# The second part of an output projection in two passes of 256 columns, with the column sums and the first FFN pair built group by group

## The chip, the cores and the metric

The kernel runs on one core of one Trainium2 chip. The metric is the device time of one execution in microseconds (us). The kernel before has a median of 2437.38 us in three runs (2435.72 to 2438.55).

The engines are called by short names: PE multiplies matrices, DVE, ACT and POOL work on tiles by element, and SP issues nearly all transfers, one after the other, in the order of the program.

## The reference, cut to what matters

One layer of a hybrid decoder, for 2048 prompt tokens and 8 decode tokens, in fp32, with a model width of 1024 and an FFN width of 2816:

```python
z = rms_norm(x, norm_mix_g) @ w_in                      # attention and convolution branches from z
...
h = x + jnp.concatenate([attn_o, conv_o], axis=-1) @ w_out
fg, fu = jnp.split(rms_norm(h, norm_ffn_g) @ w_ffn_in, 2, axis=-1)
ffn_ext = jnp.concatenate([ffn_hist.astype(fg.dtype), fg], axis=1)
fc = causal_dwconv(ffn_ext, ffn_conv_w, ffn_conv_b)
h = h + (jax.nn.gelu(fc, approximate=False) * fu) @ w_ffn_out
gate = jax.nn.sigmoid(rms_norm(h, norm_ple_g) @ w_ple_gate)
h = h + (p @ w_ple_proj) * gate
```

The change lies between `h = x + ... @ w_out` and `... @ w_ffn_in`. The norm in between needs, for each token, the sum of the squares of all 1024 entries of h: a sum over all eight blocks of 128 rows of h, which is held transposed (channels on partitions, tokens in columns).

## The kernel before, in words

**Products.** Every fp32 operand is split into a high and a low part (`hilo`, L212 to L213: ACT casts the high part, DVE subtracts it), and each product is three matmuls (L195 to L197). A weight arrives as a raw tile of 128x1024 (512 KB, L106), is split into a `whl` tile, and is used from there.

**The stream of weights.** Class `W` holds the whole sequence of weights in the order of their use. `W.topup` splits up to three weights ahead (three `whl` buffers) and loads two further ahead (two `raw` buffers). Its loads stand on SP's queue between all other loads and stores.

**Halves and columns.** The tokens are worked in two halves of 1024 columns (half 1 has 8 decode columns more). For each half, the output projection runs over columns 0 to 511 first (called the first part here, operand `mixA` or `mixB`), then over the rest, the second part. Half 0's second part is one piece of 512 columns, half 1's has pieces of 256 and 264 (`C1`).

**One unit of the second part** (`w_out_unit`, m = 0 to 7, one weight each): load the residual x (`xr`), eight times three matmuls per piece into `wo`, transpose x on PE into `xres`, copy it into `hst` (ACT), add the product (DVE, L798), store `hst` to `h` in DRAM (L806), and add its squares to the column sums `acc` (ACT squares into `sqh`, DVE adds, L816). In the last unit the squares stay apart (`tail`) and the sums take them in directly. Beside the units, `w_out_second` makes the sums of the first part: `stats` (L747 to L754: matmuls with ones, a copy, and POOL's power) at m = 0, `bcast` of the inverse root into `rb` at m = 1, and then `hn_k` for each block k: load h's columns 0 to 511 back, multiply by gain and `rb` (L773), and split into `Rb` (names `bA`, `bB`), which hold the normalised first 512 columns; `b11` keeps four of them unsplit. In half 0 the decode attention (`dec_step`) runs beside these units.

**The first part of the FFN.** The operand is taken as 2x2 blocks (rows 0 to 511 and 512 to 1023 of the normalised h; columns 0 to 511 and the rest), and the weights likewise; seven block products replace eight. Of a unit (`ffn_in`, two weights of 512 KB), `first` makes two products, X and Y, that need only `Rb`; `second` makes five, with the operands T1, T2, T3, B22 and T4, which are sums of blocks. Three of the weights are sums too, made by DVE in `topup` (L138 to L141).

`build_T` makes the five operands, once per half, for all 512 (half 1: 520) columns: loads of h into `tB` (L1120, L1122), for each k a scaling (L1134, L1138), a difference (L1135, L1139, L1143, L1150 and L1151) and a split (L1130 on ACT, L1131 on DVE): 48 DVE instructions and 20 ACT copies in all. Then come the `second` products of units 0 and 1, and units 2 to 21.

`ffn_in_all` sets the order after the last unit: `stats` and `bcast` of the last columns, `first` of units 0 and 1, `build_T`, `second` of units 0 and 1, then the units from 2 on. In half 0 a convolution (L411, DVE) fills gaps from there on (`start_conv`).

## Time and profile before

| what | us |
|---|---|
| median of three runs | 2437.38 |
| the profiled execution | 2442.29 |
| its span | 2440.5 |
| second part of the output projection, half 0 | 579.4 to 634.5 |
| first two FFN units, half 0 | 634.5 to 694.2 |
| later 20 units, half 0 | 694.2 to 1094.4 |
| second part of the output projection, half 1 | 1402.0 to 1457.0 |
| first two FFN units, half 1 | 1457.0 to 1518.7 |
| later 20 units, half 1 | 1518.7 to 1927.6 |

PE is busy for 2349.3 us of the span (96%), DVE for 1734.4 (71%), ACT for 1188.4 (49%) and POOL for 290.1 (12%). A busy time counts an instruction from its start to its end; instructions follow one another in a pipeline, so the distance from one start to the next, not the length of one, tells what one more of them costs. In a row of the timeline, the first number is the start, the second the duration, and what stands in brackets is how long the engine stood idle before and what released it. Times in the rest of the document are those of the span's clock.

### The profile page before, as it was taken

To read this page: it belongs to the slowest core of one execution; us is meant where nothing else is said; L and a number is where in the kernel's file an instruction comes from. 1 tells how busy PE (TensorE), PEld (TensorE's weight loads), DVE (VectorE), ACT (ScalarE), POOL (GpSimd) and SP (SyncE) were. 2 spreads that over 40 slices of the span, in tenths; PEclk is the share of its full clock that TensorE was granted. 3 is DMA by queue.
4 is the path that set the end of the run, shared out by engine and by line. 5 is a ranking of instruction groups with operands and counts; after the bars stand their busy time and mean duration, and the time that the engine had idled before them with its cause. 6 is when DMAs were issued, how large, how long until landed. Compare 5 with 4: busy or idle time off the path is not lost.

```text
span 2440.5 us, 36702 instructions
## 1 busy us (share of the span) xinstructions
PE 2349.3 (96%) x13709; PEld 2035.6 (83%) x13709; DVE 1734.4 (71%) x2932; ACT 1188.4 (49%) x2186; POOL 290.1 (12%) x358
## 2 busy tenths in 40 slices
PE   7899999999899999999999998999999999999999
PEld 6777778877677777778778797999999999988889
DVE  4889879856799999779944469666666654465553
ACT  4566666665444444464333345444444543344443
POOL 3312232200011121110001002111111000000000
PEclk9999999999899999999999999999999999999999
DMA  8434332267322222355556661222222665666663
GB/s 293 168 113 138 136 96 73 81 213 228 113 87 83 83 86 84 91 168 189 191 166 190 201 187 57 79 78 78 77 82 79 207 213 180 200 215 201 201 188 114
DMA packets 357076, 348.19 MB, mean 143 GB/s; under 512 B 24414, under 2 KB 277784, under 8 KB 352770
## 3 DMA queue, kind: packets, MB, share of 16 engines
q1 hardware_dynamic: 336610, 333.25, 43.4%
q10 hardware_dynamic: 20288, 12.60, 1.8%
q8 instruction: 107, 1.75, 0.3%
q14 instruction: 71, 0.58, 0.1%
HBM read 271.61 MB, written 75.78 MB: 142 GB/s over the span
## 4 chain that ended last, share of the span: by engine, by line
PE 66%; DVE 17%; DMA 8%; ACT 4%; issue 3%; POOL 2%; SPq 0%; ACTq 0%; DVEq 0%
DVE co L411 5%; PE X L195 5%; PE X L196 5%; PE X L197 5%; PE fo L197 5%; PE fo L196 5%; PE fo L195 5%; DVE whl L213 3%; PE Z L195 2%; PE Z L196 2%; PE Z L197 2%; PE pg L195 2%; PE pg L196 2%; PE pg L197 2%; PE wo L195 2%
## 5 line engine op out<-in xcount | busy, mean ns | idle before, releaser
L213 DVE TENSOR_TENSOR whl<-raw,whl 128x1024 fp32r<-128x1024 f32 (+1 forms) x314 | 361.3, 1151 | 240.7 <-ACT whl L212 240.1
L212 ACT CAST whl<-raw 128x1024 fp32r<-128x1024 f32 (+1 forms) x314 | 310.0, 987 | 257.7 <-PE fo L197 135.8
L411 DVE SCALAR_TENSOR_TENSOR co<-gi,cvec,co 128x512 f32<-128x512 f32 x480 | 367.0, 788 | 2.9
L197 PE MATMUL fo<-act,whl 128*128 128x512 f32 (+2 forms) x880 | 308.5, 351 | 2.2 <-DVE whl L213 2.1
L195 PE MATMUL fo<-act,whl 128*128 128x512 f32 (+2 forms) x880 | 308.2, 350 | 1.9 <-DVE hs L1305 1.9
L196 PE MATMUL fo<-act,whl 128*128 128x512 f32 (+2 forms) x880 | 309.0, 351 | 0.0
L197 PEld LDWEIGHTS fo<-act,whl 128*128 128x128 f32 x880 | 165.4, 188 | 19.5 <-DVE whl L213 3.3
L195 PE MATMUL X<-T,whl 128*128 128x512 f32 (+2 forms) x528 | 173.3, 330 | 8.2 <-ACT whl L212 2.5
L195 PEld LDWEIGHTS fo<-act,whl 128*128 128x128 f32 x880 | 165.4, 188 | 17.6 <-DVE hs L1305 2.3
L196 PEld LDWEIGHTS fo<-act,whl 128*128 128x128 f32 x880 | 165.6, 188 | 15.9 <-issue 0.5
L196 PE MATMUL X<-T,whl 128*128 128x512 f32 (+2 forms) x528 | 172.3, 327 | 2.6 <-DVE T L1131 2.6
L197 PE MATMUL X<-T,whl 128*128 128x512 f32 (+2 forms) x528 | 170.8, 324 | 0.6 <-DVE whl L213 0.6
L1228 POOL TENSOR_TENSOR snB<-snB 128x256 f32<-128x256 f32 (+1 forms) x66 | 87.1, 1320 | 549.4 <-ACT snB L1219 549.4
L1181 ACT ACTIVATE ft<-ft 128x512 f32<-128x512 f32 (+2 forms) x110 | 60.2, 548 | 170.3 <-DVE ft L1176 129.8
L195 PEld LDWEIGHTS X<-T,whl 128*128 128x128 f32 x528 | 100.8, 192 | 24.5 <-ACT snA L1192 6.7
L195 PE MATMUL ag<-r,whl 128*128 128x512 f32 (+2 forms) x320 | 116.5, 366 | 0.0
L196 PE MATMUL ag<-r,whl 128*128 128x512 f32 (+2 forms) x320 | 115.0, 360 | 0.0
L197 PE MATMUL ag<-r,whl 128*128 128x512 f32 (+2 forms) x320 | 113.6, 355 | 0.0
L1173 ACT ACTIVATE ft<-ext,fvec 128x512 f32<-128x512 f32 (+2 forms) x110 | 80.0, 728 | 64.6 <-DVE ext L1195 32.7
L196 PEld LDWEIGHTS X<-T,whl 128*128 128x128 f32 x528 | 101.2, 192 | 11.2 <-DVE T L1131 4.0
L197 PEld LDWEIGHTS X<-T,whl 128*128 128x128 f32 x528 | 101.2, 192 | 9.1 <-DVE whl L213 1.1
L212 ACT CAST act<-act 128x512 fp32r<-128x512 f32 (+2 forms) x110 | 56.4, 535 | 73.9 <-DMA act<-actd 72.9
(382 smaller groups left out, 6400.8 us busy)
## 6 DMA issues: line engine op xcount, KB each, us to landing
raw<-in_w_ffn_out SPq DMA_DIRECT2D x110, 512.0 KB
raw<-in_w_ffn_in SPq DMA_DIRECT2D x88, 512.0 KB
whl<-agd SPq DMA_DIRECT2D x24, 1024.0 KB
hs<-h SPq DMA_DIRECT2D x80, 256.0 KB
raw<-in_w_out SPq DMA_DIRECT2D x32, 512.0 KB
raw<-in_w_ple_gate SPq DMA_DIRECT2D x32, 512.0 KB
actd<-ft SPq DMA_DIRECT2D x44, 256.0 KB
act<-actd SPq DMA_DIRECT2D x44, 256.0 KB
```

Of the source, the lines that this page charges most:

```text
L195: PE.matmul(ps, wh, xh, start=first, stop=False, skip_group_check=more)
L196: PE.matmul(ps, wh, xl, start=False, stop=False, skip_group_check=more)
L197: PE.matmul(ps, wl, xh, start=False, stop=last, skip_group_check=more)
L212: AC.copy(hi, src)
L213: DV.tensor_tensor(lo, src, hi.bitcast(F32), op=ALU.subtract)
L411: DV.scalar_tensor_tensor(co[c], t[:, i:i + QT], cvec[:, c, i:i + 1], co[c], op0=ALU.mult, op1=ALU.add)
L1173: AC.activation(t[:, :n], ext[:, 2 + o:2 + o + n], func=AF.Identity, scale=w2, bias=bi)
L1181: AC.activation(t[:, :n], t[:, :n], func=AF.Gelu)
L1228: GP.tensor_tensor(s3, s3, s5, op=ALU.add)
```

## The change

The second part of the projection is run as two passes over all eight weights. The first pass makes columns 512 to 767 (`ga`), the second columns 768 to 1023 (`gb`, with the 8 decode columns in half 1). The weights of `w_out` stand in the stream three times per half instead of two, which is eight more loads and splits of 512 KB per half. In the first pass the residual shares the tile `hst`. The sums of `ga` are made at m = 0 of the second pass, its `bcast` at m = 1, its loads into `tB` at m = 0, and its first eight steps of the T operands (T1 and T2) from m = 2 on. `hn_k` stays in the first pass.

`build_T` becomes a class, `BuildT`, whose `step(i, o, n)` makes step i of 20 for one column group; the same 20 steps run for each group, on half the width. After the passes: sums of `gb`, `first` of units 0 and 1 over the full width, steps 8 to 15 of `ga`, the middle part of unit 0 (four products) for `ga`, steps 0 to 15 of `gb`, unit 0's middle for `gb`, steps 16 to 19 (T4) of both, unit 0's last product for both, and unit 1's `second` at full width as before. The decode steps that ran after the units of half 0 now run between the passes.

```diff
-    for _ in range(2):
+    for _ in range(3):
         for m in range(KD):
             W.add(col(w_out, m * 128))
...
+    C2 = [[(512, 256), (768, 256)], [(512, 256), (768, 264)]]
...
-        xr = xpool() if xpool else P2["st"].tile([128, STW], F32, tag="st", name="xr")
+        ho = P2["st"].tile([128, STW], F32, tag="st", name="hst")
+        if hi - lo <= 264 and not xpool:
+            xr = ho[:, RW:]
+        else:
+            xr = xpool() if xpool else P2["st"].tile([128, STW], F32, tag="st", name="xr")
...
+        ga, gb = C2[half]
         for m in range(KD):
-            w_out_unit(half, R, m, C1[half], acc, xs, xpool, tail if m == KD - 1 else None)
+            w_out_unit(half, R, m, [ga], acc, None, None, tail if m == KD - 1 else None)
             step()
...
+        if between:
+            between()
+        bt = BuildT(half, Rb, rb, b11, *where)
+        for m in range(KD):
+            w_out_unit(half, R, m, [gb], acc, xs, lambda: s2_tile("xr"), tail if m == KD - 1 else None)
+            if m == 0:
+                stats(acc, rt, *ga, tail)
+                bt.load(*ga)
+            if m == 1:
+                bcast(rt, rb, *ga)
+            for k in spread(m, 2, 8):
+                bt.step(k, *ga)
...
+        def load(self, o, n):
+            c = slice(o - 512, o - 512 + n)
+            for a, d in ((1, 0), (0, 4)):
+                for k in range(4):
+                    SY.dma_start(self.tmp[k][:, a, c], hd[self.half][k + d][:, o:o + n])
...
+            if j < 2:
+                v = (b12, b22)[j]
+                DV.scalar_tensor_tensor(v, v, gains[:, 1, k + 4 * j:k + 4 * j + 1], self.rb[:, o:o + n],
+                                        op0=ALU.mult, op1=ALU.mult)
+            if j == 0:
+                DV.tensor_tensor(t1, b12, t1, op=ALU.subtract)
+                self.split(self.T1[k], t1, c)
+            elif j == 1:
+                DV.tensor_tensor(t2, b22, t1, op=ALU.subtract)
+                self.split(self.T2[k], t2, c)
+            elif j == 2:
+                DV.tensor_tensor(b12, b22, b12, op=ALU.subtract)
+                self.split(self.T3[k], b12, c)
+            elif j == 3:
+                self.split(self.B22[k], b22, c)
+            else:
+                DV.tensor_tensor(t2, b21[:, 0, c].bitcast(F32), t2, op=ALU.subtract)
+                DV.tensor_tensor(t2, t2, b21[:, 1, c].bitcast(F32), op=ALU.add)
+                self.split(self.T4[k], t2, c)
...
-        RT = build()
+        bt.load(*gb)
+        for i in range(8, 16):
+            bt.step(i, *ga)
+        cols = [(o - 512, n, x0[-1 if i else 0], o - 512 if len(gs) == 1 else 0) for i, (o, n) in enumerate((ga, gb))]
+        u0.mid(*cols[0], bt.T2, bt.T1, bt.T3, bt.B22, True)
+        for i in range(16):
+            bt.step(i, *gb)
+        u0.mid(*cols[1], bt.T2, bt.T1, bt.T3, bt.B22, True)
+        for g in (ga, gb):
+            for i in range(16, 20):
+                bt.step(i, *g)
+        RT = bt.done()
...
+        for i, c in enumerate(cols):
+            u0.end(*c, bt.T4, i == 1)
+        u0.finish(ns)
+        for g, X in zip(gs, x1):
+            u1.second(*g, X, RT, True)
+        u1.finish(ns)
```

A scheduler places the instructions, so the order on each engine shows what the diff alone does not. On DVE in half 0, around the last residual add (the last row with `hst`; `rt` is the copy of the token sums, `ext<-Y` belongs to unit 0's `first`, `s1f` and `raw` without `whl` are weight sums), before:

```order
L213 TENSOR_TENSOR whl<-raw,whl 128x1024
L816 TENSOR_TENSOR accA<-accA,sqh 128x512
L213 TENSOR_TENSOR whl<-s1f,whl 128x512
L213 TENSOR_TENSOR whl<-raw,whl 128x512
L798 TENSOR_TENSOR hst<-hst,wo 128x512
L754 COPY rt_5549<-st 128x4
L138 TENSOR_TENSOR s1f<-raw 128x512
L139 TENSOR_TENSOR raw<-raw 128x512
L1195 TENSOR_TENSOR ext<-Y,snA 128x512
L213 TENSOR_TENSOR whl<-raw,whl 128x1024
L1134 SCALAR_TENSOR_TENSOR tB<-tB,gains,rb 128x512
```

and now (L1161 scales, L1167 makes T2's difference, L1147 splits):

```order
L802 TENSOR_TENSOR hst<-hst,wo 128x256
L213 TENSOR_TENSOR w_6894<-raw,w_6894 128x512
L213 TENSOR_TENSOR whl<-raw,whl 128x1024
L213 TENSOR_TENSOR whl<-s1f,whl 128x512
L213 TENSOR_TENSOR whl<-raw,whl 128x512
L1161 SCALAR_TENSOR_TENSOR tB<-tB,gains,rb 128x256 x2
L1167 TENSOR_TENSOR t2f<-tB,b_6303 128x256
L1167 TENSOR_TENSOR t2f<-tB,b_6309 128x256
L755 COPY rt_5549<-st 128x2
L1222 TENSOR_TENSOR ext<-Y,snA 128x512
L1147 TENSOR_TENSOR T_6500<-t2f,T_6500 128x256
L1147 TENSOR_TENSOR T_6501<-t2f,T_6501 128x256
```

The splits of unit 0's weights and the end of T2 for the first column group now stand between the last residual add and the copy of the sums; before, the copy followed the add at once.

On DVE, half 0, at the end of the T operands (`T` is T4, `ft` is the gate of unit 0), before:

```order
L1131 TENSOR_TENSOR T_6699<-t2f,T_6699 128x512
L1151 TENSOR_TENSOR t2f<-t2f,bA 128x512
L1221 TENSOR_TENSOR ext<-Z,snA 128x512
L141 TENSOR_TENSOR raw<-raw 128x512
L1131 TENSOR_TENSOR T_6700<-t2f,T_6700 128x512
L1175 SCALAR_TENSOR_TENSOR ft<-ext,fvec,ft 128x512 x2
L213 TENSOR_TENSOR whl<-raw,whl 128x1024
```

and now:

```order
L1176 TENSOR_TENSOR t2f<-t2f,bA 128x256
L1202 SCALAR_TENSOR_TENSOR ft<-ext,fvec,ft 128x256
L138 TENSOR_TENSOR s1f<-raw 128x512
L1147 TENSOR_TENSOR T_7182<-t2f,T_7182 128x256
L1203 SCALAR_TENSOR_TENSOR ft<-ext,fvec,ft 128x256
L139 TENSOR_TENSOR raw<-raw 128x512
L1202 SCALAR_TENSOR_TENSOR ft<-ext,fvec,ft 128x256
L140 TENSOR_TENSOR raw<-s1f,raw 128x512
L1203 SCALAR_TENSOR_TENSOR ft<-ext,fvec,ft 128x256
L141 TENSOR_TENSOR raw<-raw 128x512
L1258 TENSOR_TENSOR ft<-ft,X 128x256
```

The last of unit 1's weight sums, L141, stood ahead of the last split of T4; now L139 to L141 stand behind it.

On SP, half 0, where the second pass begins (`h_7` is the last block of the first pass; `tB` are the loads of h for the first column group), now:

```order
L106 DMA raw<-in_w_out 128x8x128
L810 DMA h_7_73<-hst 128x256
L1046 DMA mixB<-dOc 64x4x8
L106 DMA raw<-in_w_out 128x8x128
L1046 DMA mixB<-dOc 64x4x8
L789 DMA xr<-in_x_prompt 128x2x128
L106 DMA raw<-in_w_out 128x8x128
L1143 DMA tB<-h_0_66 128x256
L1143 DMA tB<-h_1_67 128x256
...
L789 DMA xr<-in_x_prompt 128x2x128
L106 DMA raw<-in_w_out 128x8x128
```

Where the last store of the second part was followed by the `tB` loads of 512 columns and by FFN weights, three more loads of `w_out` stand around that store now, and the next one stands behind the first group's `tB` loads.

More of the change, by code (lines that the diff above doesn't have):

```diff
@@ L180, in hybrid_layer_kernel @@
         if half:
-            for _ in range(2):
+            for _ in range(3):
                 for m in range(KD):
@@ L1076, in hybrid_layer_kernel, with w_out_second @@
     tail = {}
-    def w_out_second(half, R, acc, rt, Rb, step, xs=None, xpool=None):
+    def w_out_second(half, R, acc, rt, Rb, step, where, xs=None, between=None):
         rb = st_tile("rb")
@@ new lines, in w_out_second, with end_decode @@
+        if between:
[10 more added lines that the diff above has]
+                bt.step(k, *ga)
+        return rb, bt
+    def end_decode():
+        for _ in range(20):
+            dec_step()
+        dec_st.close()
+        RP[2] = ctx.enter_context(tc.tile_pool(name="R2", bufs=1, side="right", reuse_waits="tile"))
@@ L1242, in ffn_in, with ffn_in_all @@
         u = FfnIn()
-        u.first, u.second, u.finish = first, second, finish
+        u.first, u.second, u.finish, u.mid, u.end = first, second, finish, mid, end
         return u
-    def ffn_in_all(half, Rb, rb, acc, rt, build, ns, start=None):
+    def ffn_in_all(half, Rb, rb, acc, rt, bt, ns, start=None):
         gs = GROUPS[half]
-        stats(acc, rt, 512, sum(c for _, c in C1[half]), tail)
-        with later(72 if half else 33):
-            for o, c in C1[half]:
-                bcast(rt, rb, o, c)
+        ga, gb = C2[half]
+        stats(acc, rt, *gb, tail)
+        with later(72 if half else 60):
+            bcast(rt, rb, *gb)
         u0 = ffn_in(half, Rb, 0)
```

118 lines of the change are left out of this document (48 added, 70 removed).

## The prediction

> **What bounds the kernel now.** I read the table of engines by stretch first, over the four stretches that the change touches and the twenty FFN-in units behind each pair. Columns: length, busy time of PE, weight load, DVE, ACT, POOL, then granted clock, DMA share, GB/s.
>
> ```profile
> 579.40:634.50 55.10, 52.25 (x267) 40.67 (x265) 37.66 (x62) 29.62 (x48) 2.14 (x3) 1.00 0.71 210
> 634.50:694.20 59.70, 51.43 (x193) 36.34 (x193) 52.77 (x82) 26.69 (x44) 6.28 (x7) 0.89 0.27 85
> 1402.00:1457.00 55.00, 55.00 (x450) 53.50 (x449) 35.03 (x61) 26.63 (x53) 2.49 (x4) 1.00 0.63 191
> 1457.00:1518.70 61.70, 50.82 (x360) 46.90 (x360) 52.93 (x93) 31.76 (x61) 15.62 (x11) 0.92 0.18 54
> 694.20:1094.40 400.20, 395.49 (x1695) 315.70 (x1694) 363.95 (x518) 187.14 (x280) 63.35 (x61) 1.00 0.31 95
> 1518.70:1927.60 408.90, 406.00 (x3362) 403.67 (x3361) 258.78 (x482) 195.65 (x388) 45.35 (x79) 1.00 0.28 86
> ```
>
> Second part of the output projection (rows 1 and 3): PE nearly full at full clock, DVE 35 to 38 of 55 us, DMA at 0.63 to 0.71. First pair (rows 2 and 4): 59.7 and 61.7 us, while a later pair takes 400.2/10 = 40.0 and 408.9/10 = 40.9. So 19.7 and 20.8 us are lost, 40.5 in all; more than that cannot be won.
>
> The timeline names what ends last there: half 0, DVE from its last residual add on (start, us, then idle before and releaser in brackets), and PE at the end.
>
> ```profile
> 634.56 0.68 DVE L798 TENSOR_TENSOR hst<-hst,wo 128x512 f32<-128x512 f32 x1
> 638.96 0.16 DVE L754 COPY rt<-st 128x4 f32<-128x4 f32 x1 [3.72 <-PE st L747]
> 640.78 0.69 DVE L138 TENSOR_TENSOR s1f<-raw 128x512 f32<-128x512 f32 x1 [1.66 <-DMA raw<-in_w_ffn_in]
> 642.83 0.69 DVE L1195 TENSOR_TENSOR ext<-Y,snA 128x512 f32<-128x512 f32 x1 [0.62 <-DMA tB<-h]
> 643.85 1.23 DVE L213 TENSOR_TENSOR whl<-raw,whl 128x1024 fp32r<-128x1024 f32 x1 [0.33 <-ACT whl L212]
> ...
> 677.70 0.68 DVE L1131 TENSOR_TENSOR T<-t2f,T 128x512 fp32r<-128x512 f32 x1
> ```
>
> ```profile
> 679.02 0.50 PE L195 MATMUL X<-T,whl 128*128 128x512 f32 x1
> 694.24 0.39 PE L195 MATMUL X<-bA,whl 128*128 128x512 f32 x1
> ```
>
> DVE idles 3.72 + 1.66 + 0.62 + 0.33 = 6.3 us, then works without a gap until the last split of T4 (677.70); behind it PE needs 16 us for what is left of the first pair, and unit 2 starts at 694.24. PE meanwhile runs thin, and its clock falls:
>
> ```profile
> 650.00:660.00 10.00, 7.05 (x19) 3.62 (x17) 9.94 (x17) 4.11 (x8) 0.00 (x0) 0.79 0.00 0
> 660.00:670.00 10.00, 8.33 (x19) 5.65 (x19) 9.88 (x18) 5.71 (x11) 0.00 (x0) 0.53 0.00 0
> ```
>
> Half 1 has the same shape:
>
> ```profile
> 1457.35 0.42 DVE L798 TENSOR_TENSOR hst<-hst,wo 128x264 f32<-128x264 f32 x1
> 1497.82 0.70 DVE L1131 TENSOR_TENSOR T<-t2f,T 128x520 fp32r<-128x520 f32 x1
> ```
>
> ```profile
> 1502.09 0.58 PE L195 MATMUL X<-T,whl 128*128 128x256 f32 x1 [2.54 <-ACT whl L212]
> 1518.73 0.28 PE L195 MATMUL X<-bB,whl 128*128 128x256 f32 x1
> ```
>
> The bound of the first pair is therefore DVE's list between the last residual add and the last T4 split. The change must shorten that list, and pays in a stage where PE is full.
>
> **The list, counted.** Prices are distances between starts of back-to-back DVE instructions:
>
> ```profile
> 666.90 2.49 DVE L1131 TENSOR_TENSOR B<-tB,B 128x512 fp32r<-128x512 f32 x4
> 669.31 0.68 DVE L1151 TENSOR_TENSOR t2f<-t2f,bA 128x512 f32<-128x512 f32 x1
> ```
>
> ```profile
> 1428.39 0.41 DVE L798 TENSOR_TENSOR hst<-hst,wo 128x256 f32<-128x256 f32 x1
> 1428.72 0.75 DVE L773 SCALAR_TENSOR_TENSOR hs<-hs,gains,rb 128x512 f32<-128x512 f32 x1
> 1429.38 0.42 DVE L816 TENSOR_TENSOR accB<-accB,sqh 128x256 f32<-128x256 f32 x1
> ```
>
> A 512-wide tensor_tensor takes 2.41/4 = 0.60 us, a 256-wide one 0.33, a 512-wide scalar_tensor_tensor 0.66 (256 wide: 0.33 + 0.06 = 0.39, an estimate); a 1024-wide split 1.23 (row 643.85). In the order of instructions, before, half 0, 47 + 8 instructions of 512 and one of 1024 lie between the last residual add and the last T4 split: 47×0.60 + 8×0.66 + 1.23 = 34.7 us. Measured from the add's end (634.56 + 0.60) to the split's end (677.70 + 0.68): 43.2 = 34.7 + 6.3 idle + 2.2 small remainder. In the changed order stand there 70 tensor_tensor and 11 scalar_tensor_tensor of 256, six of 512 and two of 1024: 70×0.33 + 11×0.39 + 6×0.60 + 2×1.23 = 33.5 us. **So the list hardly gets shorter** (1.2 us): of the 96 column-group instructions that build the T operands (48 of 512 before) 18 stand ahead of the last residual add, 78 behind it; halving the rest and three weight splits that have moved behind the add take back most of what that saves. What goes is the idle: the first 9 us of the list (splits of weights, T2 of the first group, T3 steps) need no sums of the last columns, so the wait for them (3.72) and for the loads of h (0.62) is covered. New length: 33.5 + 0.3 for the add + 2.2 = 36.0, in place of 43.8 from the add's start: −7.8.
>
> Halving costs 2×0.33 − 0.60 = 0.06 us per pair here. [...]
>
> **What stands behind the list.** Before: from the split's end (678.38) 15.9 us to unit 2 in half 0. In the changed order the four weight sums of u1 (L138 to L141) end behind the last T4 split and all 60 products of u1's second lie behind u0's T4. Four gate steps and three sums: 4×0.39 + 3×0.60 = 3.4, then a cast of 1.05, together 4.4; PE then has 60 products at 0.23:
>
> ```profile
> 624.63 0.39 PE L195 MATMUL wo<-mixA,whl 128*128 128x512 f32 x1
> 624.86 0.39 PE L196 MATMUL wo<-mixA,whl 128*128 128x512 f32 x1
> ```
>
> 60×0.23 = 13.8, and 1 us for a slower clock at the start (an estimate; rows 650 to 670 show the fall): 19.2. Tail of half 0: 36.0 + 19.2 = 55.2 against 694.24 − 634.56 = 59.7: **−4.5**. Half 1: 36 + 5 (its list behind is a little longer) + 14.3 (60×2×0.119) + 1 = 56.3 against 1518.73 − 1457.35 = 61.4: **−5.1**. Sum −9.6.
>
> **The two passes.** PE's work: a 256-column unit takes 3.06 us:
>
> ```profile
> 1409.47 0.36 PE L195 MATMUL wo<-mixB,whl 128*128 128x256 f32 x1
> 1412.53 0.37 PE L195 MATMUL wo<-mixB,whl 128*128 128x264 f32 x1
> ```
>
> Half 0 has 192 products of 512 in halves: 192×(2×0.118 − 0.23) = +1 us; half 1 has pieces of this size already: 0. What is new is the weight stream: 16 weights of 512 KB per half in place of 8, each for half as long. Two raw buffers feed it. From the start of the cast to the next load's issue:
>
> ```profile
> 588.00 1.05 ACT L212 CAST whl<-raw 128x1024 fp32r<-128x1024 f32 x1 [3.52 <-PE wo L197]
> 589.08 1.23 DVE L213 TENSOR_TENSOR whl<-raw,whl 128x1024 fp32r<-128x1024 f32 x1 [3.87 <-ACT whl L212]
> 590.33 0.38 SPq L106 DMA_DIRECT2D raw<-in_w_out  x1
> ```
>
> 2.33 us. Landing of a weight with the queues light, and of a load with them full:
>
> ```profile
> 1440.37 0.38 SPq L106 DMA_DIRECT2D raw<-in_w_ffn_in  x1
> 1444.50 0.69 DVE L138 TENSOR_TENSOR s1f<-raw 128x512 f32<-128x512 f32 x1 [1.66 <-DMA raw<-in_w_ffn_in]
> ```
>
> ```profile
> 606.02 0.54 SPq L1005 DMA_DIRECT2D dmask<-in_c_dmask  x1
> 613.06 0.57 DVE L1013 CUSTOM_DVE_ANT_0 dP<-dS,dmask,dsk 64x344 f32<-64x344 f32 x1 [0.47 <-DMA dmask<-in_c_dmask]
> ```
>
> 4.13 and 7.0 us. A buffer's turn is 2.33 + landing, and brings one weight; two buffers bring one per (2.33 + landing)/2: 3.23 us light, 4.7 loaded, against PE's 3.06 to 3.1. Of the 16 weights four are there at the start, so twelve (six turns) count, from 8.6 us of stock (before: 53.3 us for the part). At 5.5 us landing, the middle, a pair of passes takes 8.6 + 6×7.83 = 55.6: +2.3; at 7.0, 8.6 + 6×9.33 = 64.6: +11.3. Half 0 moves more: 210 GB/s × 55.1 us = 11.6 MB and 4.2 new, 15.8 MB, which at the rate 210/0.71 = 296 GB/s is 53 us of 56; half 1 191×55 = 10.5 + 4.2 = 14.7 MB at 303 GB/s is 48 of 55. I take +4 in half 0 and +2 in half 1, **+6**, nearest the middle; the ends are +1 (supply keeps up) and +20 (9 and 11, loaded landing in both).
>
> The rest: eight casts and splits more per half and 16 T steps lie on ACT and DVE in the passes; DVE's instructions in the passes of half 0, at the same prices, come to some 47 of 56 us, so there is room, no price while they come in time (D). The loads of the first group's h stand in SP's queue behind h's last store and ahead of two weight loads; up to 3 us, covered by the three split weights (9 us). The decode steps between the passes only move.
>
> **Rivals.** (B) The stream keeps up: 1 − 9.6 = −8.6, to 2429 median. For it: light landing gives 3.23 against 3.06 per unit. Against: 0.71 DMA share before any of the new bytes. (C) The weight ring is at its loaded time, and PE waits for weights in both pairs: +20 − 9.6 = +10.4, to 2448, slower. It decides from where six turns cost what the tails win: 9.6/2 = 4.8 per half, landing 5.9 us or more. For it: the 7.0 us row in this very stretch. (D) The T list does not get faster: halves depend on each other through ACT, and
>
> ```profile
> 1441.52 0.41 DVE L798 TENSOR_TENSOR hst<-hst,wo 128x256 f32<-128x256 f32 x1
> 1441.97 0.42 ACT L815 ACTIVATE sqh<-hst 128x256 f32<-128x256 f32 x1 [0.57 <-DVE hst L798]
> 1442.42 0.42 DVE L816 TENSOR_TENSOR accB<-accB,sqh 128x256 f32<-128x256 f32 x1 [0.48 <-ACT sqh L815]
> ```
>
> from a DVE start to its dependent's start through ACT are 0.90 us, while the one instruction between fills 0.33. If 0.2 us stay open at 24 splits a half, 4.8 us a half are given back: the change does not do what it says, +6 − 9.6 + 9.6 = +6, about 2443. Against: the order puts several steps between.
>
> **How the numbers follow.** The profiled execution took 2442.29 us, 4.9 over the median of 2437.38. Forecast (A): +6 − 9.6 = −3.6, to 2438.7 in a profile and 2434 as median, chance 0.42, own range 2428 to 2440. B 0.26, C 0.19, D 0.13. The range 2424 to 2448 reaches to B with 5 us more (a list behind the tail that is shorter than counted) and to C's price. 0.2% is 4.9 us, about what a measurement can tell from no change. Faster by that: B and a third of A, 0.40. Same: over half of A and some of D, 0.32. Slower: C and the rest of D and A, 0.28.
>
> **What would show it.** Right: from the last residual add to the last T4 split about 36 us in place of 43.8, DVE without the 3.72 us wait on the sums, unit 2 some 55 us behind that add; the pair of passes at 55 to 57 us, with PE's waits on the split of weights (L213) some 2 to 4 us. Wrong: passes over 60 us with PE idle before each unit (C), DVE idle between T splits and released by ACT (D), or u1's products starting right behind the last T4 split.

## The result and the profile after

The changed kernel takes 2471.52 us (median of four runs, 2459.18 to 2477.93), the kernel before 2437.97 us (2435.72 to 2441.62). The ratio is 1.013, with a 95% interval of 1.0081 to 1.0179: slower by 20 to 44 us. The forecast was 2434 us, with a range up to 2448; the measured time lies outside it, on the other side. The changed kernel's runs spread more than those of the kernel before (19 us against 6), and the longer ones had the lower granted clock (a mean of 0.977 and 0.978 in the two longest, 0.984 in the shortest). Its profiled execution, 2477.77 us, is one of the two longest; that of before, 2442.29 us, was also above its median. So the two profiled executions differ by 35.5 us, and the text below explains that difference.

The table of engines by stretch, of the changed kernel: the two passes of half 0 (from the start of the first part's last residual add to the first product of the FFN), the first pair of half 0, the same two of half 1, and the twenty later units of both halves. Columns as in the prediction.

```profile
577.40:652.50 75.10, 65.96 (x478) 61.10 (x477) 48.94 (x90) 40.26 (x75) 3.10 (x5) 0.91 0.79 235
652.50:719.60 67.10, 51.74 (x242) 43.06 (x241) 60.70 (x136) 33.74 (x72) 6.56 (x9) 0.80 0.21 61
1424.00:1482.80 58.80, 54.05 (x431) 51.30 (x429) 43.31 (x76) 32.13 (x59) 2.10 (x4) 1.00 0.83 248
1482.80:1549.40 66.60, 55.54 (x361) 49.82 (x361) 56.51 (x135) 35.44 (x82) 9.32 (x13) 0.85 0.19 58
719.60:1114.80 395.20, 393.42 (x1696) 316.36 (x1695) 358.46 (x512) 185.82 (x276) 68.55 (x60) 1.00 0.31 96
1549.40:1958.70 409.30, 406.32 (x3362) 403.81 (x3361) 258.66 (x482) 195.89 (x389) 45.00 (x79) 1.00 0.28 87
```

The same table of the kernel before, with the same boundaries (the prediction's began at other products):

```profile
575.60:635.10 59.50, 56.65 (x287) 44.23 (x285) 40.18 (x66) 30.58 (x50) 2.14 (x3) 1.00 0.71 211
635.10:694.20 59.10, 50.83 (x189) 35.86 (x189) 52.17 (x81) 26.69 (x44) 6.28 (x7) 0.88 0.27 86
1404.10:1456.90 52.80, 52.80 (x432) 51.30 (x430) 33.79 (x61) 25.21 (x51) 2.49 (x4) 1.00 0.65 196
1456.90:1518.70 61.80, 50.92 (x361) 47.00 (x361) 53.03 (x93) 31.76 (x61) 15.62 (x11) 0.92 0.18 54
```

The passes cost 15.6 and 6.0 us more than the one pass did, and the first pair 8.0 and 4.8 us more: 34.4 in all. Half 0's later units take 5.0 us less (395.2 against 400.2): DVE has convolution work there (358 of 395 us busy), and what of it was done beside the longer first pair is probably not left for later. Half 1's later units take 0.4 us more. So of the 34.4 us some 29.8 stay, and the rest of the traces' difference lies in stages that the change does not touch and that vary from run to run by more (the start of the output projection lies between 505 and 517 us in the traces of this study).

What PE waits for in the passes, changed kernel: in half 0 the last mix blocks at the start (2.8 us in all), then, again and again, what its transposes of the residual (`xres`) need (5.3 us: mostly the load, in the row at 601.61 ACT's squares, as the profile has it); in half 1 nearly always the residual's loads (4.1 us).

```profile
579.79 0.51 PE L195 MATMUL wo<-mixA,whl 128*128 128x256 f32 x2 [0.96 <-ACT mixA L212]
585.43 0.62 PE L195 MATMUL wo<-mixA,whl 128*128 128x256 f32 x3 [1.82 <-ACT mixA L212]
601.61 0.41 PE L799 MATMUL xres<-ident,hst 128*128 128x128 f32 x2 [1.43 <-ACT sqh L819]
612.05 0.41 PE L799 MATMUL xres<-ident,hst 128*128 128x128 f32 x2 [0.41 <-DMA hst<-in_x_prompt]
620.78 0.41 PE L799 MATMUL xres<-ident,hst 128*128 128x128 f32 x2 [0.73 <-DMA hst<-in_x_prompt]
...
641.12 0.41 PE L799 MATMUL xres<-ident,xr 128*128 128x128 f32 x2 [1.28 <-DMA xr<-in_x_prompt]
...
1429.49 0.41 PE L799 MATMUL xres<-ident,hst 128*128 128x128 f32 x2 [0.60 <-DMA hst<-in_x_prompt]
1438.81 0.41 PE L799 MATMUL xres<-ident,hst 128*128 128x128 f32 x2 [0.79 <-DMA hst<-in_x_prompt]
1446.62 0.41 PE L799 MATMUL xres<-ident,hst 128*128 128x128 f32 x2 [1.27 <-DMA hst<-in_x_prompt]
```

No row of this list names a weight. The residual for the transposes at 612.05 was issued here, on SP's queue:

```profile
607.14 0.43 SPq L789 DMA_DIRECT2D hst<-in_x_prompt  x1
```

That is 4.9 us from issue to use (the loads and the transposes counted off in order), in units of 3.06 us; the units of 512 columns before lasted twice as long, and the kernel before shows 2.0 us of such waits in its pass of half 0 and none in half 1.

The other part of the loss in the passes of half 0 is the clock: of the 15.6 us, PE idles for 6.3 more, and is busy for 9.3 more for the same products. Windows of the changed kernel, around the stall at 585.43, around the one at 601.61, and around the one at 641.12 (with another of 1.22 us at 643.45); then windows of the kernel before at the start and near the end of its pass:

```profile
584.00:594.00 10.00, 8.57 (x48) 8.03 (x49) 4.29 (x7) 4.84 (x9) 2.11 (x2) 0.69 0.50 155
600.00:608.00 8.00, 5.68 (x37) 3.88 (x36) 6.05 (x15) 4.76 (x8) 0.00 (x0) 1.00 0.84 242
640.00:650.00 10.00, 7.66 (x39) 7.20 (x40) 8.23 (x20) 6.69 (x14) 0.00 (x0) 0.66 0.82 238
```

```profile
584.00:594.00 10.00, 9.93 (x60) 8.06 (x59) 4.42 (x6) 4.12 (x7) 2.04 (x2) 1.00 0.52 160
630.00:640.00 10.00, 10.00 (x63) 8.80 (x62) 2.06 (x4) 2.63 (x7) 0.70 (x2) 1.00 0.41 112
```

Over the passes of half 0 the granted clock is 0.91 where it was 1.00: at most 0.09 × 75.1 = 6.8 us of these 9.3, an estimate; the stalls of these passes come to 8.9 us in all. The clock does not fall behind every stall: behind the one of 1.43 us at 601.61 it stayed at 1.00, and so it did in all of half 1's passes, with stalls of up to 1.27 us. Behind the stall at 585.43 the granted clock was 0.97 from 586 to 588, 0.50 from 588 to 594, 0.82 from 594 to 596 and 1.00 from 596 to 600; products of 256 columns follow one another by 0.22 us there (590.36, 590.58) against 0.12 ahead of it (583.10, 583.21).

The first pair, on DVE and PE, changed kernel: last residual add, last T4 split, the wait behind it, and unit 2.

```profile
658.46 0.41 DVE L802 TENSOR_TENSOR hst<-hst,wo 128x256 f32<-128x256 f32 x1
...
697.75 0.41 DVE L1147 TENSOR_TENSOR T<-t2f,T 128x256 fp32r<-128x256 f32 x1
```

```profile
652.54 0.39 PE L195 MATMUL X<-bA,whl 128*128 128x512 f32 x1
...
701.54 0.58 PE L195 MATMUL X<-T,w 128*128 128x256 f32 x1 [7.30 <-DVE ft L1258]
...
719.61 0.39 PE L195 MATMUL X<-bA,whl 128*128 128x512 f32 x1
```

The list lasts from 658.46 to 698.16, 39.7 us (forecast 36.0, before 43.8), and behind it stand 21.4 us (forecast 19.2, before 15.9). But the list starts 5.9 us after PE has begun the FFN's products (652.54); before, the last add (634.56) came 0.6 us ahead of them. PE's 7.30 us wait is for a gate: the T4 product of the second column group goes into the same tile X that the first group's gate (L1258) still reads, and that gate stands behind unit 1's weight sums on DVE. The last T4 split ends at 698.16, so the last 3.4 us of the wait are the gate's.

### The profile page after: what moved, and what is told of

Read it like the earlier page. It is cut to its first block, busy times and chain, and to the rows that moved or that the text cites. A ratio compares the mean times of both kernels' runs of the same rounds, so it can differ in the third digit from the quotient of the medians.

```text
span 2475.4 us, 37597 instructions
## 1 busy us (share of the span) xinstructions
PE 2367.1 (96%) x13961; PEld 2067.7 (84%) x13961; DVE 1758.3 (71%) x3064; ACT 1214.7 (49%) x2264; POOL 290.0 (12%) x363
## 5 line engine op out<-in xcount | busy, mean ns | idle before, releaser
L213 DVE TENSOR_TENSOR whl<-raw,whl 128x1024 fp32r<-128x1024 f32 (+1 forms) x330 | 381.3, 1156 | 243.9 <-ACT whl L212 243.5
L212 ACT CAST whl<-raw 128x1024 fp32r<-128x1024 f32 (+1 forms) x330 | 326.9, 991 | 265.9 <-PE fo L197 125.1
L411 DVE SCALAR_TENSOR_TENSOR co<-gi,cvec,co 128x512 f32<-128x512 f32 x480 | 360.4, 776 | 2.8
L195 PE MATMUL X<-T,whl 128*128 128x256 f32 (+2 forms) x536 | 173.6, 324 | 8.9 <-ACT whl L212 4.5
L196 PE MATMUL X<-T,whl 128*128 128x256 f32 (+2 forms) x536 | 172.5, 322 | 0.3 <-DVE T L1147 0.3
L197 PE MATMUL X<-T,whl 128*128 128x256 f32 (+2 forms) x536 | 171.4, 320 | 0.0
L1260 POOL TENSOR_TENSOR snB<-snB 128x264 f32<-128x264 f32 (+2 forms) x67 | 92.5, 1380 | 548.8 <-ACT snB L1245 548.8
L1208 ACT ACTIVATE ft<-ft 128x256 f32<-128x256 f32 (+2 forms) x111 | 60.3, 545 | 164.1 <-DVE ft L1203 123.8
L1200 ACT ACTIVATE ft<-ext,fvec 128x256 f32<-128x256 f32 (+2 forms) x111 | 80.3, 725 | 49.7 <-DVE ext L1222 27.6
L195 PE MATMUL X<-T,w 128*128 128x256 f32 (+2 forms) x268 | 89.0, 333 | 12.4 <-DVE ft L1258 7.3
```

What stands on the lines that cost most here:

```text
L195: PE.matmul(ps, wh, xh, start=first, stop=False, skip_group_check=more)
L196: PE.matmul(ps, wh, xl, start=False, stop=False, skip_group_check=more)
L197: PE.matmul(ps, wl, xh, start=False, stop=last, skip_group_check=more)
L212: AC.copy(hi, src)
L213: DV.tensor_tensor(lo, src, hi.bitcast(F32), op=ALU.subtract)
L411: DV.scalar_tensor_tensor(co[c], t[:, i:i + QT], cvec[:, c, i:i + 1], co[c], op0=ALU.mult, op1=ALU.add)
```

## The experiments

The theory that the traces suggest (**P**): the loss is made in the passes, where a unit lasts 3 us but its inputs land as late as before (the residual 4.9 us after its issue; before, with twice the bytes, 4.9 and 6.1 in the two units of half 0's pass in which PE waited for it), and the clock falls behind stalls. Its rivals: **G**, building T by column group; **W**, the bytes of the third load of the weights; **V**, the vector work of their splits.

Ratios are to the kernel before on the same chip, with 95% intervals; the four columns behind are read from each trace as above, in us: passes and all of FFN's first part, half 0 and half 1.

| kernel | ratio | passes 0 | FFN-in 0 | passes 1 | FFN-in 1 |
|---|---|---|---|---|---|
| before | 1 | 59.5 | 459.3 | 52.8 | 470.7 |
| the change | 1.0130 (1.0081 to 1.0179) | 75.2 | 462.2 | 58.8 | 475.9 |
| passes only | 1.0108 (1.0092 to 1.0123) | 75.5 | 460.5 | 57.7 | 471.6 |
| groups only | 1.0033 (1.0017 to 1.0048) | 58.9 | 462.2 | 52.8 | 475.9 |
| own tile for the residual | 1.0122 (1.0100 to 1.0145) | 71.4 | 461.6 | 58.8 | 474.2 |
| one weight in pass 2 | 1.0021 (1.0003 to 1.0039) | 70.9 | 452.5 | 56.7 | 458.1 |
| early mix blocks | 1.0120 (1.0083 to 1.0157) | 74.0 | 462.4 | 57.4 | 474.0 |
| loads without splits | 1.0115 (1.0086 to 1.0143) | 70.0 | 463.0 | 58.7 | 467.8 |
| small loads without splits | 1.0027 (1.0010 to 1.0044) | 70.8 | 451.2 | 57.0 | 465.9 |
| no residual loads | 1.0049 (1.0031 to 1.0066) | 70.3 | 456.4 | 58.9 | 468.2 |
| no residual, early mix | 1.0016 (0.9998 to 1.0034) | 67.0 | 455.0 | 57.2 | 470.6 |
| no residual, small loads | 0.9987 (0.9974 to 1.0000) | 74.3 | 449.8 | 55.0 | 465.5 |
| filler matmuls | 1.0115 (1.0086 to 1.0144) | 77.3 | 462.7 | 58.6 | 474.8 |
| other order of the first pair | 1.0101 (1.0079 to 1.0123) | 76.7 | 458.7 | 56.7 | 471.6 |
| before, third load added | 1.0032 (1.0010 to 1.0054) | 53.4 | 463.7 | 58.1 | 476.6 |
| before, residual in the result's tile | 0.9996 (0.9975 to 1.0016) | 57.3 | 459.4 | 55.9 | 471.6 |
| one pass, sums ahead of T4 | 0.9974 (0.9956 to 0.9992) | 58.0 | 457.1 | 52.8 | 463.0 |
| the same kernel once more | 0.9979 (0.9967 to 0.9991) | 57.9 | 456.5 | 52.8 | 467.2 |
| the same, T3 on POOL | 0.9997 (0.9983 to 1.0011) | 58.3 | 456.5 | 52.8 | 470.2 |

A ratio comes from all executions, the four columns from one. Two traces of one kernel (the rows "one pass" and "the same kernel once more") differ by 4.2 us in half 1's FFN part. The trace of the change is one of its longest executions, those of "no residual loads", "loads without splits", "small loads without splits" and "other order of the first pair" are the shortest of theirs. So differences of a few us between rows say little by themselves.

**The two halves of the change apart.** Passes only: the sums, T and the first pair come behind the passes at full width.

```diff
-            if m == 0:
-                stats(acc, rt, *ga, tail)
-                bt.load(*ga)
-            if m == 1:
-                bcast(rt, rb, *ga)
-            for k in spread(m, 2, 8):
-                bt.step(k, *ga)
...
+        bt.load(512, n)
+        for i in range(20):
+            bt.step(i, 512, n)
```

> The two passes alone: 256-column passes with the third load of the weights, but sums, T operands and first pair after them at full width, as in the kernel before. Theory P (the loss is made in the passes, by residual loads and weight loads that come late and the slower clock that follows): about 20 us slower than before in the two passes (15 in half 0, 6 in half 1), tails of 59 and 61 us as before, 2455 to 2462 us in all. Rival G (the loss is made by building the T operands by column group: vector work in the second pass and behind it): within 8 us of before, 2438 to 2446 us.

Measured 2461.5 us, ratio 1.0108. Groups only: one pass of full width, two loads, and the 40 half-width steps behind it.

```diff
-    for _ in range(3):
+    for _ in range(2):
         for m in range(KD):
             W.add(col(w_out, m * 128))
...
-            w_out_unit(half, R, m, [ga], acc, None, None, tail if m == KD - 1 else None)
+            w_out_unit(half, R, m, C1[half], acc, xs, xpool, tail if m == KD - 1 else None)
...
-        for i in range(8, 16):
+        for i in range(16):
             bt.step(i, *ga)
```

> The column groups alone: one pass of 512 (520) columns with two loads of the weights, all 40 half-width steps behind it, and the first pair by group as in the change. Theory P: the passes as before; the tail has 96 half-width vector instructions in place of 48, about 3 us more a half, and the late weight sums of unit 1, another 4 us: 2445 to 2455 us, less than half of the whole loss. Rival G: most of the 33 us of the change, 2462 us or more.

Measured 2444.77 us, ratio 1.0033. The two add up: 1.08% and 0.33% are 1.41%, within the interval of the change. So three quarters of the loss come with the two passes and their third load, as P has it, and G holds for the smaller part. The table of engines of the groups-only kernel, pass and first pair of half 0, then of half 1:

```profile
575.40:634.30 58.90, 56.35 (x287) 44.29 (x286) 40.41 (x65) 30.51 (x49) 2.15 (x3) 1.00 0.70 212
634.30:703.80 69.50, 55.09 (x250) 44.83 (x250) 59.80 (x139) 33.88 (x74) 7.36 (x9) 0.80 0.25 73
1401.80:1454.60 52.80, 52.80 (x432) 51.30 (x430) 33.90 (x61) 25.54 (x51) 2.50 (x4) 1.00 0.63 196
1454.60:1520.50 65.90, 56.00 (x362) 49.59 (x362) 56.50 (x141) 34.38 (x82) 11.37 (x11) 0.87 0.17 51
```

Its first pairs take 69.5 and 65.9 us; in the change, which makes 18 of the steps inside the second pass, they take 67.1 and 66.6. What the early steps won there, the late last add took back: over all of FFN's first part the two kernels agree to 0.1 us (462.2 and 475.9 in both; that it is so close is in part chance).

**Single inputs of the passes.** A tile of its own for the first pass's residual:

```diff
-            w_out_unit(half, R, m, [ga], acc, None, None, tail if m == KD - 1 else None)
+            w_out_unit(half, R, m, [ga], acc, None, lambda: conv_p.tile([128, RW], F32, tag="gi", bufs=2, name="xrB"), tail if m == KD - 1 else None)
```

> The change, with the residual of the first pass in a tile of its own (two buffers) in place of the tile of the result. Theory P: the residual loads of the first pass are issued a unit or more earlier, its waits of some 4 us in half 0 and 3 in half 1 and a part of the half-clock stretches go: 6 to 12 us faster than the change, about 2462 us. Rival G, and a rival W (the third load of the weights sets the pace of the passes): no more than 3 us.

Measured 2466.21 us, 1.0122. The trace has 3.8 us less in half 0's passes and nothing in half 1's; the time cannot be told from the change's. PE still waits 2.0 us for these loads in half 0, and 1.5 us for splits of weights, for which it did not wait in the change. Half of what P expected, at best.

> The change, whose first pass in half 0 multiplies with mix blocks 4 and 5 in place of 6 and 7 (so half 0's columns 512 to 767 are wrong; the work is the same). It tells what the late fill of the last mix blocks costs. Theory M: the 3 us for which PE waits at the start of the first pass (a half unit reaches block 7 in 2.7 us, a full one in 5) and the half-clock stretch behind it (3 us) go: 4 to 7 us faster than the change. Rival: PE waits for the next late thing instead, the residual or a weight, 0 to 2 us.

The edit gives the first pass of half 0 the list `R[:6] + R[4:6]`. Measured 2462.1 us, 1.012, which cannot be told from the change's; the passes of half 0 get 1.2 us shorter. The rival of this one was right: PE waits for the next late thing instead. Its waits for mix blocks fall from 2.8 to 1.6 us (blocks 4 and 5 are late too), those for the residual rise from 5.3 to 7.8. Its row for the transposes that waited 1.43 us in the change:

```profile
589.81 0.66 PE L799 MATMUL xres<-ident,hst 128*128 128x128 f32 x2 [2.82 <-DMA hst<-in_x_prompt]
```

> The change with 24 matmuls of 256 columns more, unused, ahead of the first pass of half 0, on mix blocks that are there. They fill the time in which PE waits for the last mix blocks. Theory C (the stall counts twice, since the granted clock falls to 0.5 to 0.7 behind it): the added 2.8 us of matmuls cost nothing, the clock stays at 1.00 behind the start of the pass, and the passes of half 0 get 2 to 4 us shorter than 75. Rival: the clock falls at the next stall all the same; same length or up to 3 us longer.

The edit puts a product of 24 matmuls ahead of the loop. Measured 2467.09 us, 1.0115; passes of half 0 77.3 us. The wait for the mix blocks, and windows of this kernel:

```profile
582.10 0.62 PE L195 MATMUL wo<-mixA,whl 128*128 128x256 f32 x3 [1.36 <-ACT mixA L212]
```

```profile
584.00:592.00 8.00, 8.00 (x56) 7.80 (x56) 5.08 (x9) 4.50 (x9) 2.10 (x2) 0.79 0.58 179
600.00:608.00 8.00, 7.41 (x31) 4.99 (x32) 4.48 (x12) 3.53 (x5) 0.00 (x0) 0.62 0.87 260
```

The filler did not fill the stall: 1.36 us of it are left, where the change has 0.96 and 1.82. The clock still falls behind it (0.79), and falls again further on (0.62). So this kernel does not tell what the clock would do without the stall. That a lower clock is a part of the price is seen in the windows; how many us would be left without it was not isolated.

**Loads of the residual.** Left out in both passes; a resident tile is transposed in place of x, so h is wrong in those columns:

```diff
-        SY.dma_start(xr, x_p[...].rearrange("(a p) c -> p a c", p=128))
-        xsrc = [xr[:, a] for a in range(nt)]
+        if hi - lo > 264:
+            SY.dma_start(xr, x_p[...].rearrange("(a p) c -> p a c", p=128))
+        xsrc = [xr[:, a] if hi - lo > 264 else ident for a in range(nt)]
```

> The change without the loads of the residual in the two passes: it transposes and adds a resident tile in place of x, so h is wrong in those columns; sixteen loads of 128 KB per half are gone, all else stays. Theory R (in a unit half as long, the residual, which takes as long as before to land, comes late, and PE waits for it): PE's waits in front of the transposes go; the passes of half 1 fall from 59 to 53 or 54 us, those of half 0 from 75 to 66 to 70 (mix blocks and the clock behind them stay): 10 to 15 us faster than the change. Rival (something else on the in-order load queue or on DVE is late next): 5 us or less.

Measured 2452.81 us, 1.0049: about 20 us (0.8% of 2440) off the change, more than expected. But not where it was expected: half 1's passes stay at 58.9 us, and most of the gain lies in FFN's first part (5.8 and 7.7 us). The waits of PE in half 1's passes of this kernel, from the table of waits (the wait, then us in total, times, longest):

```profile
PE st L748 <- ACT sqt L808: 2.0, 1, 2.0
PE rb L761 <- POOL rt L222: 0.2, 1, 0.2
```

No wait for the residual is left; one for the squares of the first pass's last unit has come in its place, and the clock falls behind it (0.69 from 1438 to 1446). In half 0's passes of this kernel PE waits 1.7 us for casts and splits of weights. With the mix blocks early as well:

> Neither the residual's loads nor the late mix blocks 6 and 7 in the first pass of half 0 (both wrong in their result, as in the two kernels that leave out one). Theory R with theory M: both late inputs gone, no stall is left that lets the clock fall; the passes of half 0 take 60 to 63 us against 59.5 before, those of half 1 53 to 54: 16 to 22 us faster than the change. Rival: the passes of half 0 stay above 66 us.

Measured 2444.78 us, 1.0016. The time is near what was expected; half 0's passes, 67.0 us, are not: a wait of 1.8 us in the decode attention (PE's `dPTp`, behind a weight's cast on ACT) now stands where the others stood, 1.4 us of waits for mix blocks are left, and the granted clock of these passes is 0.92.

**The third load.** All eight units of the second pass on one weight:

> The change, with all eight units of the second pass on one weight: it leaves out seven loads of 512 KB, seven casts and seven splits per half, so the weights of the second pass are wrong. Rival W: the second passes run at the PE's pace, 10 to 20 us faster than the change. Theory P (residual loads and vector work, not the weights, are late): 2 to 8 us faster, mostly for 8 us of vector splits less per half.

Measured 2439.01 us, 1.0021: 27 us off the change, which seems to decide for W. It does not, since the stream of weights then runs on: FFN's first weights are loaded and split inside the pass, and the list behind the last add falls to 31.6 us. So the stream was kept in step, with all loads and only the first split per half:

```diff
+                if kind == "load":
+                    W.raws.pop(i)
+                    hl = W.kept
...
-            W.add(col(w_out, m * 128))
+            (W.add if p < 2 or m == 0 else W.add_load)(col(w_out, m * 128))
```

> The change, which loads all eight weights of the second pass but splits only the first of them, so the second pass is wrong from unit 1 on; it leaves out seven casts (ACT) and seven splits (DVE) per half, not the loads. Set against the kernel with one weight (32 us faster than the change). Theory V (vector work: 8 us of splits a half stand in the list that ends last): 25 us or more faster than the change, as without the loads. Rival W (the transfers): 10 us or less.

Measured 2465.86 us, 1.0115. V does not hold: 14 casts and splits per kernel less give 4 us by the ratios, within the intervals. The same with an eighth of each load:

```diff
-                    SY.dma_start(dst, src)
+                    k = 1 if kind == "load" else src.shape[1]
+                    SY.dma_start(dst[:, :k], src[:, :k])
```

> As the kernel that loads the weights of the second pass and does not split them, with an eighth of each load (64 KB of 512): seven times 448 KB less per half, the same number of loads in the same order. Theory R: the bytes are not what is late; within 3 us of that kernel. Rival W (the bytes of the third load): 8 us or more faster than it.

Measured 2447.77 us, 1.0027: 0.9% or 21 us less than with full loads, for 3.1 MB a half, as W expected. Yet the passes are hardly shorter (70.8 and 57.0); the gain is in FFN's first part (451.2 against 463.0 in half 0). The rows of DVE tell why. Full loads, no splits, behind the last residual add of half 0:

```profile
641.68 0.41 DVE L810 TENSOR_TENSOR hst<-hst,wo 128x256 f32<-128x256 f32 x1
642.01 0.68 DVE L221 TENSOR_TENSOR w<-raw,w 128x512 fp32r<-128x512 f32 x1
643.46 1.23 DVE L221 TENSOR_TENSOR whl<-raw,whl 128x1024 fp32r<-128x1024 f32 x1 [0.76 <-ACT whl L220]
644.60 0.68 DVE L221 TENSOR_TENSOR whl<-s1f,whl 128x512 fp32r<-128x512 f32 x1
645.20 0.68 DVE L221 TENSOR_TENSOR whl<-raw,whl 128x512 fp32r<-128x512 f32 x1
```

Small loads:

```profile
637.51 0.69 DVE L222 TENSOR_TENSOR w<-raw,w 128x512 fp32r<-128x512 f32 x1
639.58 0.42 DVE L811 TENSOR_TENSOR hst<-hst,wo 128x256 f32<-128x256 f32 x1
643.58 0.42 DVE L811 TENSOR_TENSOR hst<-hst,wo 128x256 f32<-128x256 f32 x1
645.53 0.16 DVE L764 COPY rt<-st 128x2 f32<-128x2 f32 x1 [0.51 <-PE st L757]
```

With the small loads the splits of FFN's first weights stand ahead of the last residual add; with full ones four of them stand behind it, in the list that ends last. This order is the program's own, made before the run; that the scheduler goes by when it expects a load to land is inferred from this pair. So, by this pair, the bytes of the third load cost mainly through FFN's first weights, whose splits move past the end of the passes, and not by starving the passes.

Does the third load cost without half units? In the kernel before, with a second, unused load beside each weight of the second part:

> The kernel before with a second load of 512 KB beside each of the eight weights of the second part (eight more per half, as in the change; loaded into the same two buffers, not split, not used). It prices the third load alone, without half units. Theory R (the bytes are not what is late; half units reach their inputs too soon): within 5 us of before. Rival W (16 loads through two buffers in the time of eight units, and FFN's first weights behind them): 12 to 20 us slower than before.

Measured 2449.72 us, 1.0032: 8 us, between the two expectations; W alone is worth a quarter of the loss. (Half 0's pass reads short in this trace, as the last transposes and the decode attention's last products stand behind the FFN's first product there.) In half 1 PE waits once, 2.6 us, for the residual, in units of full width. The residual in the result's tile, in the kernel before:

> The kernel before with the residual of the second part loaded into the tile of the result, as in the first pass of the change, in units of full width. Theory R: a full unit gives the load 6 us, the loads land in 4 to 5: 0 to 6 us slower than before. Rival: the shared tile by itself, whatever the width, makes the loss: 10 us or more.

Measured 2440.73 us, 0.9996: the shared tile alone costs nothing that can be measured in the time. In its trace PE waits for the residual once for 1.4 us in half 1, whose pass is 3.1 us longer, and 0.2 us in half 0. So half units are not the only thing that can make the residual late: the third load or the shared tile does it too, though for fewer units.

Last, both large causes left out in one kernel:

> The change with neither the residual's loads in the two passes nor full weight loads and splits in the second pass (both results wrong, as in the two kernels that leave out one). If the two causes are separate, their gains add up: 20 + 27 us off the change, 2420 to 2430 us, faster than before. If both are one shortage of the same in-order queue and its transfers, the second removal adds little to the first: 2438 to 2448 us, about as the kernel with small loads alone.

Measured 2438.4 us, 0.9987. Without the residual the change gets 20 us faster, with small loads and no splits 25 us, with both 35 us: less than the sum, 45, and more than either. They share a part; which, the runs do not tell, since small loads move the splits of FFN's first weights (one stands behind the last residual add of half 0 in place of five), and the missing residual leaves them there but takes the list down from 39.7 to 35.3 us, nearly all of it DVE's idle time. The passes of half 0 are not short in this kernel either (74.3 us); its FFN part is (449.8). The row of these passes:

```profile
576.10:650.50 74.40, 68.12 (x484) 64.64 (x482) 48.54 (x101) 35.84 (x75) 2.19 (x5) 0.86 0.58 170
```

The granted clock of 0.86 is worth up to 0.14 × 74.4 = 10.4 us of them, an estimate. The longest waits of PE left are 1.9 us in the decode attention, 1.4 us for the split of a weight and 1.2 us for mix blocks. So in half 0 neither the residual's loads nor the bytes of the third load are needed for long passes: other waits come in their place. In half 1 the passes do come down, from 58.8 to 55.0 us (52.8 before).

**The first pair.** The change with unit 1's sums ahead of the T4 steps, and both T4 products ahead of the gates:

```diff
         u0.mid(*cols[1], bt.T2, bt.T1, bt.T3, bt.B22, True)
+        W.topup(5)
...
+        for c in cols:
+            u0.prod4(*c, bt.T4)
         for i, c in enumerate(cols):
-            u0.end(*c, bt.T4, i == 1)
+            u0.end(*c, bt.T4, i == 1, True)
```

> The change, with unit 1's weight sums and their splits ahead of the T4 steps, and both of unit 0's T4 products ahead of its gates. Theory S (behind the last T4 split PE waits for the sums of unit 1 and, in half 0, for the gate of the first column group, which reads the same tile): the stretch from the last T4 split to unit 2 falls from 21 and 22 us to 16 to 18, the list grows by up to 3.5 us in each half (three sums and the splits go ahead): 2 to 8 us faster in all. Rival: the list ends last in any order and grows by what stands behind it less; no change within 2 us.

Measured 2460.08 us, 1.0101: 7 us less by the ratios, at the upper end of what was expected, though the intervals overlap. FFN's first part falls by 3.5 and 4.3 us. Nearly the same order in the kernel before, with one pass and T at full width (unit 0's four middle products and then unit 1's sums ahead of the T4 steps):

> The kernel before with one reordering: one pass, two loads of the weights, T at full width, but unit 0's first four second products and then unit 1's weight sums ahead of the T4 steps. Theory S: PE's wait of 2.5 us and more behind the last T4 split in half 1 goes, 2 to 4 us faster than before in half 1, nothing in half 0: 2433 to 2437 us. Rival: the list is only rearranged: 2436 to 2441 us.

Measured 2428.98 us, 0.9974; the same kernel measured again:

> The one-pass kernel with unit 1's weight sums ahead of the T4 steps, measured again in more rounds: 0.995 to 0.999 of before, as at first (0.9974).

Measured 2435.61 us against 2441.49, 0.9979 (0.9967 to 0.9991). This one is faster than the kernel before, by 5 to 6 us. The wait of 2.54 us that the kernel before has at 1502.09 for ACT's cast of unit 1's sums stands behind its last T4 split; here PE waits for a weight's cast for 1.58 us, at 1484.96, ahead of the last T4 split (1495.22), and behind it only after unit 2 has begun (1.55 us, at 1508.63). The trace's row where unit 2 starts, early, among what is left of unit 1:

```profile
1498.50 0.28 PE L195 MATMUL X<-bB,whl 128*128 128x256 f32 x1
```

One further step on that kernel, T3's four differences on POOL (`GP.tensor_tensor` in place of `DV.tensor_tensor`):

> The one-pass kernel with unit 1's sums ahead of T4 (2429 us), with T3's four differences on POOL in place of DVE, and T3 behind B22. Theory L (DVE's list ends last in the first pair): four times 0.6 us a half off the list, 2 to 5 us faster than that kernel, 0.994 to 0.997 of before. Rival: POOL, slower by a factor of about four per element, becomes what T3 waits for: no change or up to 4 us slower than it.

Measured 2439.46 us, 0.9997 (0.9983 to 1.0011): no gain over before, so the 5 us are gone again, though the intervals overlap. That fits the rival: POOL took 1.82 us for each of the four (in the kernel before, its 22 sums of 512 columns take 2.15 in the mean), where DVE starts the next instruction of this size after 0.60.

## Why the prediction was wrong, point by point

**What bounds the first pair**, DVE's list from the last residual add to the last T4 split, fits the runs. In the groups-only kernel, 96 half-width instructions in place of 48 full ones and the new order of unit 0's products and unit 1's sums make the pair longer by 10.4 and 4.1 us, with no loss in its pass; how much each of the two costs was not separated.

**The tails, "−4.5" and "−5.1".** From the last residual add to unit 2 they took 61.2 us in half 0 and 61.5 in half 1, against 59.7 and 61.4 before: +1.5 and +0.1. In half 0 the list came down by 4.1 us where 7.8 were forecast; its work was counted rightly. DVE's idle rows in it, changed kernel:

```profile
666.54 1.22 DVE L213 TENSOR_TENSOR whl<-raw,whl 128x1024 fp32r<-128x1024 f32 x1 [1.26 <-ACT whl L212]
...
672.90 0.42 DVE L1147 TENSOR_TENSOR B<-tB,B 128x256 fp32r<-128x256 f32 x1 [1.39 <-ACT B L1146]
...
683.89 0.42 DVE L1247 TENSOR_TENSOR ext<-Z,snA 128x256 f32<-128x256 f32 x1 [0.62 <-PE Z L197]
...
687.15 0.76 DVE L1147 TENSOR_TENSOR T<-tB,T 128x256 fp32r<-128x256 f32 x2 [1.17 <-ACT T L1146]
```

4.4 us, of which 2.6 are hand-overs from a cast on ACT to a half-width split (rival D's mechanism), where the sum had 2.2 for all remainders. What stands behind it grew by 5.5, where 3.3 were forecast: the step that priced unit 1's sums was right (4.4 us of DVE and cast; from 698.16 to 702.23 they took 4.1), the gate in the shared tile was not seen. And the start of the list was taken as given: the steps put into the second pass, the residual adds and the weight splits queue on DVE, so the last add comes 5.9 us behind PE's first FFN product. In the passes-only kernel, without these steps, it comes 0.1 us behind.

**The passes, "I take +4 in half 0 and +2 in half 1"**: this is the step that failed. By the boundaries of the forecast (last add to last add) they came to +22.2 and +10.7; by PE's first FFN product, +15.6 and +6.0. Of the 38.1 us between the forecast (−3.6) and what the trace shows by the same boundaries (+34.5), 26.9 lie in the passes and 11.2 in the tails. Products of half the width follow one another by 0.12 us, as forecast. But the sum priced one input of a unit, its weight, by the turn of the two raw buffers (from a stock of 8.6 us that it does not work out), and in the change PE never waited for it. It called the queues light where a weight landed in 4.13 us; the DMA engines were 70% busy in that stretch (1440.0 to 1444.5). It had no term for the other two inputs: the mix blocks, of which a half unit reaches the last in half the time (2.8 us of waits in half 0), and the residual, which lands 4.9 us after its issue, in units of 3.06 (5.3 us of waits in half 0, 4.1 in half 1). And none for the clock: up to 6.8 us in half 0. These are the waits that the change's trace shows; the kernels that take one of them out show other waits in its place, so the wrong term is not one late input but that none but the weight was looked at. The third load did its harm elsewhere, in the arrival of FFN's first weights, which the sum had counted as "three weight splits that have moved behind the add" and not as a consequence of the load.

**The rivals.** C had the sign and nearly the sum of the passes (+20 against +21.6 by PE), by another mechanism: the price was right by chance, since in the change the weight ring was not what PE waited for (where other inputs are taken out, it is so for 1.5 to 2.1 us). D was a part of what happened in the list. That the list "hardly gets shorter" in work was right, and should have weighed more: where the work does not shrink, a gain has to come from idle time alone, and 6.3 us of that were all there was.

**The range** left out that several late inputs of a stage in which PE is busy for 95% or more of the time add up (56.65 of 59.5 us and 52.8 of 52.8 before), and it took each cost as if the others were free.

What stays open: how much of the 20 us of the residual's loads is their lateness and how much the scheduler's other order, since every edit here lets it place other instructions too; and how many us the falling clock costs by itself, and why it falls behind some stalls and not behind others.

## What to carry to other kernels

When a unit of work is cut in half, list every input of the unit, not only the largest, and compare each one's time from issue to landing with the new length of the unit; to keep the same lead in time, a load has to be issued twice as many units ahead. A stage in which PE is full has little slack for stalls of one or two us: in the passes of half 0 PE's idle time went from 2.9 us to 9.1, and behind some of the stalls the clock fell as well (to 0.50 from 588 to 594). And when one late input is taken out, look for the next one before counting the gain. An early start of dependent work is worth only the idle time that it fills; if it stands on the engine that is late already, it delays the work that everything waits for.

## What the runs showed of the hardware

In half 0's passes the stall of 1.82 us, and those of 1.28 and 1.22 us, which follow each other closely, were each followed by several us at a granted clock well below 1 (0.69 and 0.66 over windows of 10 us; 0.50 from 588 to 594 and from 643 to 649). The stall of 1.43 us at 601.61 was not (1.00 from 600 to 608), nor were those of up to 1.27 us in half 1's passes (1.00 throughout). A residual tile of 128 KB took 4.9 us from issue to use with the DMA engines 95% busy (607.1 to 612.05), no less than the weight of 512 KB that the prediction quotes (4.13 us, with the DMA engines 70% busy). So a quarter of the bytes did not land sooner here. At 256 KB, in half 0's pass of the kernel before, the residual took 4.9 and 6.1 us from issue to use (602.10 to 607.01 and 607.67 to 613.75), with a DMA share of 1.04 and 1.09 in the table of engines.
